# Reordering the even block's mixer: the recurrence's projections first, the attention beside the recurrence

## The chip, the cores and the metric

The kernel runs on one core of one Trainium2 chip, in one launch. The metric is the device time of a launch in microseconds (us), from the core's own clock. The profile is of one execution; its views give times from the start of that execution's span.

## The reference, cut to what matters

The program is a stack of blocks on 256 tokens of width 1024, in float32: a first block (attention beside a state-space mixer, then a feed-forward over 16384 experts), then two further layers. The change touches the mixer of the first of those two, the "even" one:

```python
def even_mixer(h, h_ctx, w_in, w_out, rpb, lb, hg_norm_w, with_ctx_out):
    na_q, na_k, na_v, hg_q, hg_ff, hg_fb, hg_i, hg_g = jnp.split(h @ w_in, EV_SPLITS, axis=-1)
    cna_q, cna_k, cna_v, chg_q, chg_ff, chg_fb, chg_i, chg_g = jnp.split(h_ctx @ w_in, EV_SPLITS, axis=-1)
    a_lat = neighbourhood_attention(nh(na_q), nh(na_k), nh(na_v), nh(cna_k), nh(cna_v), rpb)
    g_lat, g_ctx = hgrn2_mixer(hg_q, (hg_ff, hg_fb), hg_i, hg_g,
                               chg_q, (chg_ff, chg_fb), chg_i, chg_g, lb, hg_norm_w, with_ctx_out)
    y = jnp.concatenate([a_lat.reshape(b, s, NA_WIDTH), g_lat], axis=-1) @ w_out
```

So one wide projection (1024 to 4096 columns, in eight slices of 512) of the tokens `h` and of a 256-token context `h_ctx` feeds two branches that do not need each other: an attention of 8 heads of 64 (each query sees a window of the tokens plus all of the context), and a gated linear recurrence of 4 heads of 128, run once forward and once backward (d = 0 and 1). Both branches' outputs, side by side, go through the output projection.

## The kernel before, in words

**Projections.** Weights come from memory in units of 512 KB (128 rows x 1024 float32). Each unit is split into a high part (ScalarE, L217) and a low part (VectorE, every third one GpSimd, L222), and each product is three passes of matmuls, high by high, high by low and low by high (L227 to L229). `ev_in(c0, puts)` (L1409) does one 512-column slice that starts at column c0: two loads of two units each, and for each load and each source (`h`, or `hc` for the context) two groups of 24 matmuls of 256 columns; after each such pair of groups it yields. A slice wanted of both sources yields four times, a slice wanted of `h` alone twice. Group results leave PSUM (two buffers named mm) by the function `put`: a copy, a gate (`gate_T`: ScalarE tanh, VectorE L1402), or a silu (L1407).

The slices by their first column: 0 attention query (naq), 512 attention key (done ahead of the order that changes, with `first_T`), 1024 attention value, 1536 recurrence query (hq), 2048 and 2560 forget gates forward and backward, 3072 recurrence value (iv, civ), 3584 output gate (gN).

**Attention.** `nattn` (L1431) is a generator of 16 tiles, 8 heads by 2 halves of the tokens. A tile has scores (matmuls L1452, L1453), a bias added from PSUM to the tile s (L1455), a maximum (L1458), ScalarE's exponential (L1460), a reciprocal (L1461), four transposes (L1468), their copy to pT (L1470), the product with the values (L1474), and a scaling (L1475). Each head's bias is read by four DMAs of 64 KB on GpSimd's queue into braw, one buffer (L1441), and masked on GpSimd into bias, two buffers (L1443).

**Recurrence.** `prep` (L1533) makes, for each direction d and each pair of heads pc, the decays: logarithm, a scan along time (L1503), differences, exponentials and products (L1508 to L1518), and 8 transposes (L1529). `hgrn` (L1549) then works through 8 steps, head by head and in each head d = 0 and 1: `states` (matmuls L1557, L1570, L1573, VectorE L1559 and two scans L1577 of 512 columns) and, one step later, `outputs` of the step before (matmuls L1597 and 32 small ones L1602; after d = 1 also a normalisation: some 12 small VectorE operations from L351 on, and L1616). `by_chunk` (L1583) spreads a head's values on GpSimd (L1588) into two tiles that carry the attention's names s and pT, so they share the attention's two buffers each.

**Output projection.** `out_att(tt)` (L1673) starts the sum for half tt of the tokens from the residual (L1676) and adds the attention's four units `ua`; the recurrence's four units `ub` come last, with the next norm. Both halves' sums stay in PSUM (four buffers named acc, which the attention's scores and values and the recurrence's states use too). Units of the output weights are first multiplied by a gate row on GpSimd (L275).

**What sets the order.** Every engine has one queue and works it in order. The order written in the program gives priorities; a planner lays out each engine's queue from them with its own estimate of when operands and buffers are ready, so an instruction that is written later can stand ahead of one that would wait (the attention's first scores stand among the value projections that are written before them). SyncE's queue carries the weight loads, GpSimd's the bias loads.

The order written before: slices 0 and 1024 complete; then slices 2048, 3072, 2560, 1536 and 3584, sixteen yields, with one or two attention tiles after each of the first twelve, the decays after yields 4 to 6 and 12 to 15, and the first two recurrence steps after yields 14 and 15. At yield 11 the attention is finished, and its tiles naq and nak (and cnak, cnav) are reused for the transposed mixer outputs mixA and mixH. The other six recurrence steps follow with `out_att(0)` among them, then `out_att(1)` and the rest:

```python
    for i, _ in enumerate(units):
        for _ in range(2 if i % 3 == 2 else 1):
            next(na, None)
        if 4 <= i <= 6 or i >= 12:
            next(pr, None)
```

Of the kernel before, what the change touches and what calls it, by code (L numbers as in the profile page):

```python
# [8 lines left out]
F32 = mybir.dt.float32  # L9
F32R = mybir.dt.float32r  # L10
# [7 lines left out]
D = 1024  # L18
# [66 lines left out]
def program(tc, I, out, C, taps=None, upto=99):  # L85
# [1306 lines left out]
    def copy_T(dst, scale=1.0):  # L1392
        def put(ps, i):
            S.activation(dst[:, i], ps, AF.Copy, scale=scale)
        return put

    def gate_T(d, which):
        def put(ps, i):
            o = F[:, d, i // 2, which, i % 2]
            S.activation(o, ps, AF.Tanh, scale=0.5)  # L1400
            j = d * 4 + i
            V.tensor_scalar(o, o, lbc[:, 2, j:j + 1], lbc[:, 1, j:j + 1], op0=OP.mult, op1=OP.add)  # L1402
        return put
# [5 lines left out]
    def ev_in(c0, puts, natural=False):  # L1409

        for pc in range(2):
            un = load_up(Wev, c0 + pc * 256)
            for hsrc, put in puts:
                for u in range(2):
                    ps = ps_mm()
                    if natural:
                        up_N(un, u, hsrc, ps)
                        put(ps, u, slice(pc * 256, pc * 256 + 256))
                    else:
                        up_T(un, u, hsrc, ps)  # L1420
                        put(ps, pc * 2 + u)
                yield

    def copy_N(dst):
        return lambda ps, tt, cs: S.activation(dst[:, tt, cs], ps, AF.Copy)
# [123 lines left out]
    def hgrn(mixH):  # L1549
        def states(hd, d):  # L1550
            pc, hh = hd // 2, hd % 2
            kdl, kdc = KD[d, pc]
            kk, qe = F[:, d, pc, 0, hh], LF[d][:, pc, 1, hh]
            pa = ps_tr((128, 2, 128))
            for tt in range(2):
                ts = slice(tt * 128, tt * 128 + 128)
                P.matmul(pa[:, tt], kk[:, ts], qe[:, ts], start=True, stop=True)  # L1557
            at_ = atb[d][hd % 2]
            V.copy_predicated(at_, mdir[d].unsqueeze(1).to_broadcast([128, 2, 128]), pa)  # L1559

            st_ = []
            et = wrk.tile([128, 512], F32, name="et")
            S.activation(et.rearrange("p (v n) -> p v n", n=8), tots[d][pc][:, hh].unsqueeze(1).to_broadcast([128, 64, 8]),
                         AF.Exp)
            for vh in range(2):
                vs = slice(hd * 128 + vh * 64, hd * 128 + vh * 64 + 64)
                pm = ps_acc()
                pu = pm.rearrange("p (v n) -> p n v", n=8)
                for tt in range(2):
                    P.matmul(pu[:, 0], kdc[:, tt, hh], civ[:, tt, vs], start=tt == 0, stop=tt == 1)  # L1570
                for m, tt in enumerate((1, 0) if d else (0, 1)):
                    im = ivm[hd][tt][:, vh * 64:vh * 64 + 64]
                    P.matmul(pm.rearrange("p (v n) -> p v n", n=8)[:, :, 4 * m + 1:min(4 * m + 5, 8)], kdl[:, tt, hh],  # L1573
                             (im[:, :, 3:0:-1] if m else im[:, :, ::-1]) if d else (im[:, :, 0:3] if m else im),
                             start=True, stop=True)
                sv = wrk.tile([128, 512], F32, name="sv", bufs=3)
                V.tensor_tensor_scan(sv, et, pm, 0.0, op0=OP.mult, op1=OP.add)  # L1577
                st_.append(sv.rearrange("p (v n) -> p n v", n=8))
            return hd, d, at_, st_, qe

        oN, ivm, last_out = {}, {}, hg_out

        def by_chunk(hd):  # L1583

            ivm[hd] = []
            for tt, name in enumerate(("s", "pT")):
                t = wrk.tile([128, 512], F32, name=name).rearrange("p (v n) -> p v n", n=4)
                G.tensor_tensor(t, iv[:, tt, hd * 128:hd * 128 + 128].unsqueeze(2).to_broadcast([128, 128, 4]),  # L1588
                                rmask.unsqueeze(1).to_broadcast([128, 128, 4]), op=OP.mult)
                ivm[hd].append(t)  # L1590

        def outputs(hd, d, at_, st_, qe):
            if d == 0:
                oN[hd] = ps_mm((128, 2, 128))
            o = oN[hd]
            for tt in range(2):
                P.matmul(o[:, tt], at_[:, tt], iv[:, tt, hd * 128:hd * 128 + 128], start=d == 0 and tt == 0, stop=False,  # L1597
                         skip_group_check=True)
            for vh in range(2):
                for n in range(8):  # L1600
                    tt, i = n // 4, n % 4
                    last_out[0] = P.matmul(  # L1602
                             o[32 * i:32 * i + 32, tt, vh * 64:vh * 64 + 64], qe[:, n * 32:n * 32 + 32],
                             st_[vh][:, 7 - n if d else n], start=False, stop=d == 1 and vh == 1 and n == 7,
                             skip_group_check=True, tile_position=(0, 32 * i))
            if d == 0:
                return
            ss = wrk.tile([128, 2], F32, name="ss4")
            scr = wrk.tile([128, 512], BF, name="junk")
            for tt in range(2):  # L1610
                S.activation(scr[:, 0:128], o[:, tt], AF.Square, accum_out=ss[:, tt:tt + 1])
            rsqrt(ss, 1.0 / 128, 4 * EPS)
            cs = slice(hd * 128, hd * 128 + 128)
            ms = slice(512 + hd * 128, 640 + hd * 128)
            for tt in range(2):
                V.scalar_tensor_tensor(mixn[:, tt, ms], o[:, tt], ss[:, tt:tt + 1], gN[:, tt, cs], op0=OP.mult, op1=OP.mult)  # L1616

        last = None
        by_chunk(0)
        for hd in range(4):  # L1620
            if hd < 3:
                by_chunk(hd + 1)
            for d in range(2):
                if hd % 2 == 0:
                    queries(d, hd // 2)
                new = states(hd, d)
                if last:
                    outputs(*last)
                    if d == 0:
                        nat_T(lambda tt, c: mixn[:, tt, (4 + hd - 1) * 128:(4 + hd) * 128],  # L1630
                              [t[:, hd - 1:hd] for t in mixH], 1)
                last = new
                yield
        outputs(*last)
        yield True
        nat_T(lambda tt, c: mixn[:, tt, 896:1024], [t[:, 3:4] for t in mixH], 1)
# [1 line left out]
    first_T(1, hc, cnak)  # L1638
    first_T(0, h, nak)
    first_T(1, h, nak)  # L1640
    for g in (ev_in(0, [(h, copy_T(naq, 0.125))]),
              ev_in(1024, [(hc, copy_N(cnav)), (h, copy_N(nav))], True)):
        for _ in g:
            pass
    na, pr = nattn(), prep()
    units = itertools.chain(
        ev_in(2048, [(hc, gate_T(0, 1)), (h, gate_T(0, 0))]),
        ev_in(3072, [(hc, copy_N(civ)), (h, copy_N(iv))], True),
        ev_in(2560, [(hc, gate_T(1, 1)), (h, gate_T(1, 0))]),
        ev_in(1536, [(h, lambda ps, i: silu(hq[:, i], ps))]),  # L1650
        ev_in(3584, [(h, gate_N)], True))
    hg = mixA = None
    hg_out = [None]
    for i, _ in enumerate(units):
        for _ in range(2 if i % 3 == 2 else 1):
            next(na, None)
        if 4 <= i <= 6 or i >= 12:
            next(pr, None)
        if i == 11:
            for _ in na:  # L1660
                pass
            mixA = (mt([128, 4, T], "naq", F32R), mt([128, 4, T], "nak", F32R))
            mixH = (mt([128, 4, T], "cnak", F32R), mt([128, 4, T], "cnav", F32R))
            hg = hgrn(mixH)
        if i == 14:
            nat_T(lambda tt, c: mixn[:, tt, c * 128:(c + 1) * 128], mixA, 4)
        if i >= 14:
            next(hg)
    Weo = I["ev_w_out_2"][0]
    ua = load_dn(Weo, 0, grow, 4)  # L1670
    acc = [None, None]
# [7 lines left out]
            yield  # L1679

    o0 = out_att(0)
    for i, tail in enumerate(hg):
        if i < 6:
            next(o0, None)
        if i == 2:
            hh2, hl2 = mt([128, 2, D], "hh", F32R), mt([128, 2, D], "hl", F32R)
            ub = load_dn(Weo, 4, grow, 4, [(hh2[:, 0], hl2[:, 0]), (hh2[:, 1], hl2[:, 1])])
        if i == 6:
            for _ in o0:
                pass  # L1690
        if tail:
            with tc.issue_after(hg_out[0].ins):
                for _ in out_att(1):
                    pass
# [44 lines left out]
```

## Time and profile before

| what | value |
|---|---|
| median of 3 runs | 2160.7 us (2158.08 to 2161.99) |
| the profiled execution's own time | 2161.18 us |
| its span, first to last instruction | 2159.4 us |
| TensorE matmul busy | 2058.1 us (95%) |
| VectorE busy | 1607.4 us (74%) |
| ScalarE busy | 1030.4 us (48%) |
| GpSimd busy | 795.1 us (37%) |
| mean granted TensorE clock | 0.983 |

Reading: PE is TensorE's matmuls, PEld its weight loads, DVE VectorE, ACT ScalarE, POOL GpSimd, SP SyncE. L12 is line 12 of the kernel. Matmuls are pipelined, so the busy time of PE counts overlapping durations, and the distance from start to start says more about its pace. The mixer in question runs from about 1365 to 1645 us of the span.

### The profile page before, as it was taken

How to read it: one execution, taken by the hardware profiler on the slowest of the kernel's cores; microseconds unless marked ns; L12 is line 12 of the kernel's file. 1: busy time of each engine (PE TensorE's matmuls, PEld its weight loads, DVE VectorE, ACT ScalarE, POOL GpSimd, SP SyncE). 2: the span in 40 equal slices, each digit the busy share in tenths (PEclk: the TensorE clock that was granted, in tenths of full speed). 3: DMA queues.
4: the chain of work that ended last, by engine and by line, in shares of the span. 5: the costliest groups of instructions: out<-in, count | busy, mean ns of one | idle time of the engine just before them, and what ended most of it. 6: DMA issues, size and time to landing. Idle time of an engine off the chain costs nothing.

```text
span 2159.4 us, 37426 instructions
## 1 busy us (share of the span) xinstructions
PE 2058.1 (95%) x14726; PEld 1898.8 (88%) x14726; DVE 1607.4 (74%) x2576; ACT 1030.4 (48%) x1732; POOL 795.1 (37%) x392
## 2 busy tenths in 40 slices
PE   8999999999879999999999999999888999899999
PEld 7989999889879999997777777899876999798998
DVE  6677688779999346758997787536785877777877
ACT  5655565454434444444444555435524545445454
POOL 2221333113957876550000000323441556343554
PEclk9999999999989999999999999999999999899999
DMA  6544544456645766559998888746224655554552
GB/s 218 159 127 135 169 128 128 133 201 200 220 138 189 231 211 189 173 174 328 349 331 318 314 280 256 166 97 76 89 69 141 194 199 181 181 171 144 193 182 98
DMA packets 122035, 403.56 MB, mean 187 GB/s; under 512 B 14561, under 2 KB 23793, under 8 KB 121858
## 3 DMA queue, kind: packets, MB, share of 16 engines
q1 hardware_dynamic: 110688, 388.43, 54.4%
q0 software_dynamic: 1520, 3.75, 2.7%
q10 hardware_dynamic: 9650, 8.99, 1.2%
q8 instruction: 115, 1.88, 0.4%
q14 instruction: 62, 0.51, 0.1%
HBM read 390.56 MB, written 10.55 MB: 186 GB/s over the span
## 4 chain that ended last, share of the span: by engine, by line
PE 68%; DVE 17%; DMA 8%; issue 3%; ACT 3%; POOL 0%; SPq 0%; DVEq 0%; ACTq 0%; POOLq 0%
PE mm L227 15%; PE mm L228 14%; PE mm L229 14%; PE acc L309 4%; PE acc L312 4%; PE acc L308 4%; DMA xdt<-in_ada_w 3%; DMA wraw<-in_peer_v 3%; DVE A L180 3%; DVE wlo L1064 3%; PE tr L1019 1%; PE acc L1019 1%; DVE wlox L222 1%; DVE wlo L222 1%; ACT whi L1063 1%
## 5 line engine op out<-in xcount | busy, mean ns | idle before, releaser
L1043 POOL TENSOR_TENSOR wlo<-wraw,whi 128x1024 fp32r<-128x1024 f32 x126 | 321.3, 2555 | 182.6 <-ACT whi L1042 182.4
L227 PE MATMUL mm<-xdt,whi 128*128 128x256 f32 x1248 | 360.7, 290 | 7.1 <-ACT A L1055 5.7
L229 PE MATMUL mm<-xdt,wlo 128*128 128x256 f32 x1248 | 355.0, 285 | 0.6 <-POOL wlo L1043 0.6
L228 PE MATMUL mm<-xdt,whi 128*128 128x256 f32 x1152 | 327.9, 285 | 0.2 <-DVE xdt L418 0.2
L1042 ACT ACTIVATE whi<-wraw 128x1024 fp32r<-128x1024 f32 x128 | 135.7, 1060 | 236.0 <-PE mm L228 152.2
L227 PEld LDWEIGHTS mm<-xdt,whi 128*128 128x128 f32 x1248 | 240.5, 193 | 8.6 <-ACT A L1055 6.3
L229 PEld LDWEIGHTS mm<-xdt,wlo 128*128 128x128 f32 x1248 | 241.0, 193 | 1.4 <-POOL wlo L1043 1.2
L228 PEld LDWEIGHTS mm<-xdt,whi 128*128 128x128 f32 x1152 | 223.1, 194 | 0.4 <-DVE xdt L418 0.4
L222 POOL TENSOR_TENSOR wlo<-wraw,whi 128x1024 fp32r<-128x1024 f32 x37 | 93.8, 2538 | 308.4 <-ACT whi L217 271.6
L1063 ACT ACTIVATE whi<-wraw 128x1024 fp32r<-128x1024 f32 x128 | 134.6, 1057 | 106.8 <-DMA wraw<-in_peer_v 100.5
L1064 DVE TENSOR_TENSOR wlo<-wraw,whi 128x1024 fp32r<-128x1024 f32 x128 | 155.5, 1220 | 23.1 <-ACT whi L1063 22.9
L222 DVE TENSOR_TENSOR wlo<-wraw,whi 128x1024 fp32r<-128x1024 f32 x87 | 134.9, 1551 | 46.7 <-ACT whi L217 46.3
L227 PE MATMUL mm<-F,whix 128*128 128x256 f32 x560 | 158.6, 284 | 7.1 <-ACT whix L217 5.0
L217 ACT ACTIVATE whi<-wraw 128x1024 fp32r<-128x1024 f32 x124 | 130.7, 1055 | 71.9 <-PE mm L228 42.4
L228 PE MATMUL mm<-F,whix 128*128 128x256 f32 x560 | 158.5, 283 | 0.4 <-DVE F L418 0.4
L229 PE MATMUL mm<-F,wlox 128*128 128x256 f32 x560 | 158.2, 283 | 0.5 <-DVE wlox L222 0.5
L309 PE MATMUL acc<-wlo,wwh 128*128 128x512 f32 x512 | 149.9, 395 | 6.6 <-DVE wlo L1064 6.4
L312 PE MATMUL acc<-whi,wwl 128*128 128x512 f32 x512 | 147.2, 394 | 5.6 <-DVE wwl L222 5.4
L308 PE MATMUL acc<-whi,wwh 128*128 128x512 f32 x512 | 141.5, 393 | 5.5 <-ACT whi L1063 5.2
L275 POOL TENSOR_TENSOR wrawx<-wrawx,grow 128x1024 f32<-128x1024 f32 x38 | 107.0, 2828 | 90.5 <-DMA wrawx<-in_ffn_w_down 47.0
L1382 POOL MEMSET att<- 128x256 f32 x4 | 1.2, 312 | 358.2 <-DVE xdt L180 358.2
L309 PEld LDWEIGHTS acc<-wlo,wwh 128*128 128x128 f32 x512 | 95.5, 189 | 32.3 <-DVE wlo L1064 12.6
(619 smaller groups left out, 6321.6 us busy)
## 6 DMA issues: line engine op xcount, KB each, us to landing
wraw<-in_peer_u SPq DMA_DIRECT2D x128, 512.0 KB
wraw<-in_peer_v SPq DMA_DIRECT2D x128, 512.0 KB
xdt<-in_ada_w SPq DMA_DIRECT2D x72, 512.0 KB
wraw<-in_ffn_w_up SPq DMA_DIRECT2D x56, 512.0 KB
wraw<-in_w_in SPq DMA_DIRECT2D x42, 512.0 KB
wrawx<-in_ffn_w_up SPq DMA_DIRECT2D x32, 512.0 KB
wrawx<-in_ffn_w_down SPq DMA_DIRECT2D x31, 512.0 KB
wrawx<-in_w_in SPq DMA_DIRECT2D x30, 512.0 KB
```

The source lines that it names most:

```text
L217: S.activation(hi, raw, AF.Copy)
L222: eng.tensor_tensor(lo, raw, hi.bitcast(F32), op=OP.subtract)
L227: P.matmul(ps, ah, bh, start=start, stop=False)
L228: P.matmul(ps, ah, bl, start=False, stop=False)
L229: P.matmul(ps, al, bh, start=False, stop=stop)
L308: P.matmul(acc[tt][hf], ah, hi[:, fs], start=st_, stop=False, skip_group_check=free)
L309: P.matmul(acc[tt][hf], ah, lo[:, fs], start=False, stop=False, skip_group_check=free)
L312: P.matmul(acc[tt][hf], al, hi[:, fs], start=False, stop=sp_ and not free, skip_group_check=free)
L1042: S.activation(hi, raw, AF.Copy)
L1043: (G if b in POOL_U else V).tensor_tensor(lo, raw, hi.bitcast(F32), op=OP.subtract)
L1063: last_hi[0] = S.activation(hi, raw, AF.Copy)
L1064: V.tensor_tensor(lo, raw, hi.bitcast(F32), op=OP.subtract)
```

## The change

The slices are written in another order: 2048, 2560, 3072, 1024, 1536, 0, 3584, so that what the recurrence needs comes first, and the attention's query last but one. That is 22 yields (0 to 21). The decays stand after yields 4, 6, 8 and from 16 on; the first two recurrence steps stand after yields 19 and 21. The attention starts only behind the projections: four times one recurrence step and four attention tiles. Then the attention's output is transposed, and the last two recurrence steps run with `out_att(0)` between them; `ub` is loaded right behind `ua`.

Three things go with it. `by_chunk` gets tiles of its own (iv0, iv1), in place of the attention's s and pT. mixH lies in the tile of the context's low part (hcl), in place of cnak and cnav. And the room that is set aside for the descriptors of GpSimd's DMAs is set to 4096 bytes of each partition.

```diff
-            for tt, name in enumerate(("s", "pT")):
-                t = wrk.tile([128, 512], F32, name=name).rearrange("p (v n) -> p v n", n=4)
+            for tt in range(2):
+                t = wrk.tile([128, 512], F32, name=f"iv{tt}").rearrange("p (v n) -> p v n", n=4)
...
-    for g in (ev_in(0, [(h, copy_T(naq, 0.125))]),
-              ev_in(1024, [(hc, copy_N(cnav)), (h, copy_N(nav))], True)):
-        for _ in g:
-            pass
     na, pr = nattn(), prep()
-    units = itertools.chain(
...
+    for i, _ in enumerate(itertools.chain(
+            ev_in(2048, [(hc, gate_T(0, 1)), (h, gate_T(0, 0))]),
+            ev_in(2560, [(hc, gate_T(1, 1)), (h, gate_T(1, 0))]),
+            ev_in(3072, [(hc, copy_N(civ)), (h, copy_N(iv))], True),
+            ev_in(1024, [(hc, copy_N(cnav)), (h, copy_N(nav))], True),
+            ev_in(1536, [(h, lambda ps, i: silu(hq[:, i], ps))]),
+            ev_in(0, [(h, copy_T(naq, 0.125))]),
+            ev_in(3584, [(h, gate_N)], True))):
+        if 4 <= i < 10 and i % 2 == 0 or i >= 16:
+            next(pr, None)
+        if i == 18:
+            mixH = mt([128, 2, 4, T], "hcl", F32R)
+            mixH = (mixH[:, 0], mixH[:, 1])
+            hg_out = [None]
+            hg = hgrn(mixH)
+        if i >= 19 and i % 2:
+            next(hg)
+    for _ in pr:
+        pass
+    for i in range(4):
+        next(hg)
+        for _ in range(4):
             next(na, None)
...
+    for _ in na:
+        pass
+    mixA = (mt([128, 4, T], "naq", F32R), mt([128, 4, T], "nak", F32R))
+    nat_T(lambda tt, c: mixn[:, tt, c * 128:(c + 1) * 128], mixA, 4)
     Weo = I["ev_w_out_2"][0]
     ua = load_dn(Weo, 0, grow, 4)
...
     o0 = out_att(0)
-    for i, tail in enumerate(hg):
-        if i < 6:
-            next(o0, None)
-        if i == 2:
-            hh2, hl2 = mt([128, 2, D], "hh", F32R), mt([128, 2, D], "hl", F32R)
-            ub = load_dn(Weo, 4, grow, 4, [(hh2[:, 0], hl2[:, 0]), (hh2[:, 1], hl2[:, 1])])
-        if i == 6:
+    hh2, hl2 = mt([128, 2, D], "hh", F32R), mt([128, 2, D], "hl", F32R)
+    ub = load_dn(Weo, 4, grow, 4, [(hh2[:, 0], hl2[:, 0]), (hh2[:, 1], hl2[:, 1])])
+    for tail in hg:
+        next(o0, None)
+        next(o0, None)
+        if tail:
             for _ in o0:
                 pass
-        if tail:
             with tc.issue_after(hg_out[0].ins):
...
-    nc = bacc.Bacc("TRN2", target_bir_lowering=False, num_devices=1)
+    nc = bacc.Bacc("TRN2", target_bir_lowering=False, num_devices=1, dynamic_dma_scratch_size=4096)
```

## Rows read from the trace of the kernel before

**Rows 1.** Busy time by stretch: us; PE, PEld, DVE, ACT, POOL busy (count); granted clock, DMA share, GB/s

```profile
1420.00:1430.00 10.00, 10.00 (x86) 10.00 (x85) 0.52 (x1) 2.46 (x5) 2.14 (x1) 1.00 0.33 105
1450.00:1540.00 90.00, 89.72 (x692) 83.21 (x690) 55.80 (x91) 47.62 (x85) 23.74 (x25) 1.00 0.49 71
1540.00:1590.00 50.00, 37.47 (x250) 34.72 (x249) 47.95 (x46) 20.64 (x34) 38.78 (x20) 0.90 0.38 119
1590.00:1637.00 47.00, 45.50 (x465) 37.13 (x464) 31.54 (x83) 10.19 (x29) 3.49 (x3) 1.00 0.03 10
```

**Rows 2.** Who waited for whom, 1375 to 1650 us: total, times, longest

```profile
PE mm L227 <- DVE hq L1407: 3.6, 2, 3.3
PE tr L1529 <- DVE e L1515: 3.6, 1, 3.6
```

**Rows 3.** Line L227 alone, by stretch: PE and PEld busy (count)

```profile
1450.00:1540.00 90.00, 46.45 (x160) 30.18 (x160) 1.00 0.49 71
```

**Rows 4.** The chain that ended last, 1360 to 1680 us: start, us, what

```profile
1440.95 0.84 PE acc L1474 x8
...
1447.54 0.63 PE acc L1452 x2
1448.17 0.43 PE acc L1453 x2
...
1454.09 0.44 PE tr L1468 x4
...
1590.95 0.44 PE tr L1557 x4
...
1598.19 0.39 PE acc L1570 x4
1598.58 0.81 PE acc L1573 x4
...
1608.84 1.07 PE mm L1602 x32
...
1630.90 1.91 PE acc L1676 x4
...
1637.91 0.47 PE acc L312 x2
```

**Rows 5.** VectorE's groups by line, 1370 to 1660 us: busy, mean ns, idle before

```profile
L222 DVE TENSOR_TENSOR wlo<-wraw,whi 128x1024 fp32r<-128x1024 f32 x19 | 28.9, 1519 | 18.9 <-ACT whi L217 18.9
L1577 DVE TENSOR_TENSOR_SCAN sv<-et,acc 128x512 f32<-128x512 f32 x16 | 19.3, 1214 | 4.3 <-PE mm L1602 3.5 <-PE acc L1573 0.6
...
L1470 DVE COPY pT<-tr 128x512 f32<-128x512 f32 x16 | 10.9, 683 | 1.8 <-PE tr L1468 1.7
L1458 DVE TENSOR_REDUCE nm<-s 128x1 f32<-128x512 f32 x16 | 10.8, 678 | 1.5 <-ACT s L1456 1.4
L1455 DVE TENSOR_TENSOR s<-acc,bias 128x256 f32<-128x256 f32 x16 | 6.7, 419 | 3.3 <-PE acc L1453 3.3
L1475 DVE TENSOR_SCALAR n<-acc,sm 128x64 f32<-128x64 f32 x16 | 4.5, 279 | 11.3 <-PE acc L1474 11.3
L1461 DVE RECIPROCAL sm<-sm 128x1 f32<-128x1 f32 x16 | 2.6, 160 | 7.1 <-ACT s L1460 7.1
```

**Rows 6.** VectorE in order of time, 1597 to 1602 us: start, us, what

```profile
1597.57 0.14 DVE L351 TENSOR_SCALAR ss<-ss 128x2 f32<-128x2 f32 x1
...
1600.94 0.61 DVE L1616 SCALAR_TENSOR_TENSOR n<-mm,ss,gN 128x128 f32<-128x128 f32 x2
```

**Rows 7.** Line L1515 alone: duration ns min/median/max, first and last start

```profile
L1515 DVE TENSOR_TENSOR e<-e,F x4: 1225/2462/3357, 1470.1 to 1571.5; 128x1024 f32<-128x1024 f32 x4
```

**Rows 8.** The tile braw: duration ns min/median/max, first and last start; landing

```profile
L1441 POOL DMA_DIRECT2D braw<-in_na_rpb x32: 619/619/631, 1361.4 to 1501.3; - x32
L1443 POOL TENSOR_TENSOR bias<-braw,win x8: 1279/1282/1286, 1373.9 to 1511.1; 128x512 f32<-128x512 f32 x8
...
DMA to landing us min/median/max: 4.1/7.2/10.4
```

More of the change, by code (lines that the diff above doesn't have):

```diff
@@ L1640, in program @@
     first_T(1, h, nak)
-    for g in (ev_in(0, [(h, copy_T(naq, 0.125))]),
-              ev_in(1024, [(hc, copy_N(cnav)), (h, copy_N(nav))], True)):
-        for _ in g:
-            pass
     na, pr = nattn(), prep()
-    units = itertools.chain(
[L1647 to L1655, printed above, removed]
-            next(na, None)
[L1657 to L1668, printed above, removed]
+    for i, _ in enumerate(itertools.chain(
[20 more added lines that the diff above has]
+        for _ in range(4):
+            next(na, None)
+    for _ in na:
+        pass
+    mixA = (mt([128, 4, T], "naq", F32R), mt([128, 4, T], "nak", F32R))
+    nat_T(lambda tt, c: mixn[:, tt, c * 128:(c + 1) * 128], mixA, 4)
     Weo = I["ev_w_out_2"][0]
```

## The prediction

> **What bounds the kernel now.** I read the busy times by stretch first. From 1391 us (the end of the key projection, where the order begins to differ) to 1540 TensorE is full: 1420 to 1430 shows what full is, 86 starts of projection matmuls in 10 us, 0.116 us each, and 1450 to 1540 shows it with attention tiles and half the decays mixed in [rows 1]. Those 90 us hold 3 x 160 projection matmuls [rows 3], 55.8 us, and the other 212 instructions are 12 attention tiles and 16 transposes with four strays. At the prices of the chain [rows 4] a tile is 0.63 + 0.43 + 0.44 + 0.84 = 2.34 us, 28.1 us for 12, and the transposes 1.8 us: 85.7 of 90 us, so TensorE works at 95%. VectorE is busy for 62% there.
>
> Then it turns over. [...] The waits name it: TensorE waits 3.6 us for VectorE's silu of hq and 3.6 us for its product in the decays [rows 2]. [...] From 1590 to 1637 neither is full of work: the recurrence steps follow one another, VectorE at 67%, and TensorE's 45.5 busy us contain overlapping durations. Priced as below, its work there (8 sets each of L1557, L1597 and L1602, 10 pairs of L1570 and L1573, 51 matmuls like L312, 6 of L1676) is 42.5 us, 90%. The last matmul of `out_att(1)` ends at 1638.4 [rows 4]. So VectorE's work is badly spread: little before 1540, too much after.
>
> **The change part by part.** Nothing is removed or added in arithmetic; the sum is the length of the stretch from 1391 to 1638.4, now 247.4 us, in three parts.
>
> *Projections.* 22 yields of 48 matmuls at 0.116 us are 122.8 us. Beside them stand all 32 decay transposes (3.5 us at L1468's price), two `states` and one `outputs`. A `states` is 0.44 + 2 x (0.39 + 0.81) = 2.84 us of TensorE; an `outputs` is 0.44 (L1597, four of the form of L1557) + 1.07 = 1.51 [rows 4]. Together 133.5 us; at the 95% above 140.5, to 1531.5. VectorE's work for these (splits, gates, four decays) filled 62% or less of the like stretch; the backward decays need the last context product, at yield 14, and have eight yields of 5.6 us to run in before the end. What covers them is that room; if they came late, the stalls of [rows 2] would return, 7 us. Weight loads: the last six yields take 6 MB in 34 us, of which the four raw buffers can hold 2 MB beforehand; the other 4 MB are 119 GB/s, what 1540 to 1590 moved at 0.38 of the DMAs' time [rows 1]. I take no stall.
>
> *Attention beside four recurrence steps.* TensorE: 16 x 2.34 + 4 x 4.35 = 54.8 us, 57.7 at 95%. VectorE [rows 5]: a tile is 0.42 + 0.68 + 0.16 + 0.68 + 0.28 = 2.22 us, 35.5 for 16; four `states` at 2 x 1.21 + 0.42 (L1559, taken at L1455's price: as many columns from PSUM) are 11.4; two normalisations from 1597.57 to 1601.55 with a scan of 1.2 between, 2.8 each [rows 6], 5.6; two query products at 0.68 (512 columns, as L1458), up to 2.5 each beside GpSimd; four splits of `ua` at 1.52, 6.1. That is 60 us bare. The attention's and the scans' operations, which read PSUM or one SBUF operand, are not slowed by GpSimd in the trace; for the others I add 3.6 us: 63.6, and at the 96% busy that VectorE reached from 1540 to 1590, 66 us. Ends: 57.7 (TensorE alone at 95%) and 73 (TensorE at its 75% of 1540 to 1590). I take 66, because VectorE's sum is the larger. To 1597.5. A tile that slips in among the last projections costs there what it saves here, and is not counted.
>
> *The tail.* Two `states` and three `outputs`, 10.2 us; 16 transposes for mixA and mixH, 1.8; both `out_att`: 48 matmuls at 0.235 and eight of the residual, 3.8 [rows 4], 15.1. Sum 27.1; at the 90% of 1590 to 1637, 30 us. To 1627.6. The ends are 27 and 36 (TensorE at 75%).
>
> The sum is 236.6 against 247.4: 10.8 us less. What comes behind (the recurrence's output units, the norm) only moves along.
>
> *Small parts.* The tiles of `by_chunk` are what lets steps and attention overlap; their GpSimd work is the same. mixH in the context's tile waits for yield 14's products, which are long done. The smaller room for descriptors could at worst make each of GpSimd's loads wait for the one before, 4 x 7.2 us a head in place of 4 x 0.62 [rows 8]; four loads are outstanding at most, as before, and no row shows an issue that waited, so I take 0 and leave a chance for it. At the start, GpSimd's bias loads before the first split may be gone or not: 0 to 1.5 us of gain, taken as 0.
>
> A sentence on the clock: the stretch from 1590 to 1637, all small matmuls and transposes, was granted 1.00 [rows 1]. [...]
>
> **The rivals.**
> *A, no change.* The two branches are chained through the same four acc buffers, freed by VectorE in queue order; TensorE then gets no more than its 75% in the last two parts: 73 + 36 = 109 in place of 96, the end at 1640, 2163 us. For it: TensorE and VectorE are both near full. Against: at 95% with attention among projections they shared those buffers too.
>
> *B, slower: the bias loads become the bound.* braw is one buffer, so a head's bias takes four issues, the landing and the mask: 2.5 + 7.2 + 1.3 = 11.0 us at the median, 7.9 to 14.2 by the landing's ends [rows 8]. Now the eight masks are spread over 1373.9 to 1511.1, some 20 us apart; behind the change eight heads get 66 us, 8.2 each. Two masked heads and one raw lie ready; the mask of head 2 comes when head 0 is done, 8.2 us in, and head 7's is then 8.2 + 5p, wanted at 57.7 us. At p = 11.0 it is 5.5 us late, at 14.2 it is 21.5 late: 2172 us. It decides from p = 12.1, where it eats the 10.8 us. `ua`'s gate products in GpSimd's queue add to p. Against it: the DMAs have little else to do, so landings should lie at the short end.
>
> *C, better: everything overlaps.* 97% on TensorE in the first part, 58 us in the second, 28 in the tail: 2139 us. For it: VectorE has room during the last projections.
>
> [...]
>
> That the change doesn't reorder what it says isn't likely: every engine works its queue in order, though the planner, not the written order, has the last word on how far the attention moves.
>
> **How the numbers follow.** Forecast 0.51, A 0.16, B 0.19, C 0.12, D 0.02. The profiled execution took 2161.18 us, span 2159.4 and 1.8 around it, 0.5 above the median of 2160.7. Less 10.8 it is 2150.4; I give 2151. Range: the forecast's own ends run from 2142 (the second part at its lower end) to 2156; A reaches 2163, and the milder half of B, up to a period of 12.8, adds 14.5 to the forecast, 2165; C is mostly below. 2140 to 2166 leaves out D, half of B and most of C. What a measurement can tell here is about 0.2%, 4.3 us: faster below 2156.4, slower above 2165. Faster: forecast and C, 0.63; same: A, 0.16; slower: B and D, 0.21.
>
> **What would show it.** Right: projections back to back from 1391 to about 1531, with all four L1503 scans inside; no stretch of 50 us with VectorE at 96% while TensorE is below 80%; L1515 nearer 1.2 us; attention scores L1452 among recurrence L1573 up to some 1597; the last `out_att` at about 1628. Wrong by A: TensorE idle behind pT, sv or s in the middle part. Wrong by B: GpSimd's L1443 waiting for braw instead of for L1455, and L1455 waiting for bias. A stall for hq or the splits before 1531 would say that the cover of the decays failed.

## The result, and the profile after

The changed kernel took 2187.7 us (median of 4, 2180.47 to 2194.48) against 2159.39 us (median of 4): a ratio of 1.0132 with a 95% interval of 1.0089 to 1.0176. It is slower by 1.3%, where 2151 us was forecast. The profiled execution took 2194.48 us, span 2192.7, granted clock 0.971; it is the longest of the four, which took 2180.47, 2182.71, 2192.69 and 2194.48 us at mean clocks of 0.980, 0.978, 0.973 and 0.971.

The first part ended when forecast. TensorE in order of time, in the kernel after: the last matmul of a projection stands at 1532.3 us, where 1531.5 was forecast.

```profile
1532.32 0.28 PE L229 MATMUL mm<-whi,hl 128*128 128x256 f32 x1
1532.44 0.61 PE L1597 MATMUL mm<-iv,att 128*128 128x128 f32 x4
```

Busy time by stretch, in the columns of [rows 1]:

```profile
1450.00:1532.00 82.00, 81.32 (x659) 79.24 (x658) 45.84 (x46) 39.50 (x61) 33.80 (x16) 1.00 0.37 117
1540.00:1590.00 50.00, 33.61 (x167) 26.49 (x168) 30.59 (x62) 9.28 (x25) 20.61 (x21) 0.58 0.47 47
1590.00:1637.00 47.00, 43.87 (x243) 35.34 (x242) 24.17 (x60) 11.73 (x31) 8.69 (x11) 0.68 0.28 12
1540.00:1650.00 110.00, 89.33 (x454) 71.88 (x455) 59.81 (x133) 22.98 (x61) 29.30 (x32) 0.61 0.35 31
```

TensorE is full to 1532, with VectorE at 56%. Then two things are to be seen. From 1540 to 1590 VectorE is busy for 30.59 of 50 us, not the 47.95 of [rows 1], so the heap of VectorE's work is gone, as meant; but TensorE issued 167 instructions in place of 250. And the granted clock is 0.58 and 0.68. Read in stretches of 2 us from 1540 to 1650, it is 1.00 or 0.50, and between them (0.70 to 0.94) only where it goes from one to the other. With these as the upper and the lower level, a mean of 0.61 over 110 us is, as an estimate, 2 x 0.39 x 110 = 86 us at the lower one; the kernel before, at 0.95 over the same stretch, had 11.

TensorE's waits from 1375 to 1680 us (total, times, longest), the counterpart of [rows 2], show one that is new:

```profile
PE tr L450 <- DVE n L1616: 13.3, 1, 13.3
PE acc L1474 <- DVE pT L1470: 7.3, 10, 0.8
PE mm L1602 <- DVE sv L1577: 2.7, 3, 1.8
...
PE tr L1529 <- DVE e L1515: 1.1, 2, 0.8
```

The waits for hq and e have shrunk to 0.4 and 1.1 us. The new one is a stop of 13.3 us behind the first normalisation. VectorE in order of time there (start, us), beside [rows 6], where L351 took 0.14 us:

```profile
1541.09 2.31 DVE L351 TENSOR_SCALAR ss<-ss 128x2 f32<-128x2 f32 x1
1543.43 0.65 DVE L354 TENSOR_SCALAR rq<-ss 128x2 int32<-128x2 int32 x1
...
1544.32 0.16 DVE L357 SCALAR_TENSOR_TENSOR rq<-ry 128x2 f32<-128x2 f32 x1
1544.51 6.63 DVE L358 TENSOR_TENSOR rq<-rq,ss 128x2 f32<-128x2 f32 x1
1551.06 1.21 DVE L222 TENSOR_TENSOR hl<-wraw,hh 128x1024 fp32r<-128x1024 f32 x1
...
1552.58 0.16 DVE L358 TENSOR_TENSOR rq<-rq,ss 128x2 f32<-128x2 f32 x1
```

and GpSimd in the same microseconds, without a gap:

```profile
1540.01 3.36 POOL L275 TENSOR_TENSOR wraw<-wraw,grow 128x1024 f32<-128x1024 f32 x1
1543.33 0.72 POOL L1429 TENSOR_TENSOR gN<-gN,nw 128x256 f32<-128x256 f32 x1
1544.00 2.46 POOL L1441 DMA_DIRECT2D braw<-in_na_rpb  x4
1546.47 2.35 POOL L275 TENSOR_TENSOR wrawx<-wrawx,grow 128x1024 f32<-128x1024 f32 x1
1548.77 2.35 POOL L275 TENSOR_TENSOR wraw<-wraw,grow 128x1024 f32<-128x1024 f32 x1
```

L358 multiplies two elements a partition. It ends at 1551.14, within 0.02 us of the end of GpSimd's last gate product, and 6.63 us is 41 times what it takes at 1552.58. The transposes L450 and L1468, on TensorE's queue behind it, waited, to 1554.04 and 1554.31.

Last, the clock. Six stretches between 1555 and 1650 us, in the same columns:

```profile
1555.00:1574.00 19.00, 17.55 (x62) 14.29 (x61) 7.22 (x15) 2.78 (x7) 3.73 (x5) 0.50 0.27 13
...
1583.00:1598.00 15.00, 14.22 (x51) 11.50 (x50) 6.57 (x24) 2.71 (x8) 5.33 (x8) 0.50 0.64 27
1600.00:1609.00 9.00, 8.22 (x76) 6.29 (x74) 5.54 (x13) 3.22 (x8) 3.10 (x5) 1.00 0.20 13
1610.00:1622.00 12.00, 12.00 (x43) 10.46 (x44) 4.57 (x10) 2.01 (x5) 1.27 (x1) 0.50 0.36 14
1623.50:1629.00 5.50, 5.03 (x57) 3.82 (x56) 4.04 (x15) 2.72 (x9) 0.00 (x0) 1.00 0.01 3
1630.00:1649.50 19.50, 17.58 (x66) 14.28 (x66) 7.64 (x22) 3.94 (x10) 0.00 (x0) 0.50 0.08 27
```

The chain that ended last, from 1605 to 1631:

```profile
1605.06 0.60 PE tr L1468 x4
...
1605.69 0.70 DVE pT L1470
...
1606.44 1.10 PE acc L1474 x8
...
1608.60 0.60 PE tr L1468 x4
...
1609.23 0.70 DVE pT L1470
...
1609.97 1.97 PE acc L1474 x8
...
1618.60 1.60 PE acc L1573 x4
...
1624.35 0.44 PE tr L1468 x4
...
1628.57 0.70 DVE pT L1470
...
1629.32 1.78 PE acc L1474 x8
```

Two attention tiles in a row sent their transposes and then waited 0.70 us for the copy to pT; L1474 behind the second is at the lower level, 1.97 us for the 1.10 of 3.5 us before. From there to 1622.5 the chain stays on TensorE without a wait, with a recurrence step in it at double price (L1573 1.60 against 0.81 of [rows 4]), and L1468 at 1624.35 is at the upper level again. At 1628.6 a wait for pT stands in the chain once more, and from 1630 the clock is at 0.50. So in this trace the clock falls among attention tiles and comes back with each recurrence step, at about 1575, 1599, 1623 and 1650. Of the 86 us at the lower level some 34 run from the stop at 1541 to the end of the next recurrence step, at 1574.6; the other 50, in three stretches that begin at 1582, 1610 and 1629.5, follow on waits for pT of 0.8 us at most, with no stop before them.

### The profile page after: what moved, and what is told of

It reads as the page before. It is cut to its first block, busy times and chain, and to the rows that moved or that the text cites. A ratio compares the mean times of both kernels' runs of the same rounds, so it can differ in the third digit from the quotient of the medians.

```text
span 2192.7 us, 37443 instructions
## 1 busy us (share of the span) xinstructions
PE 2081.4 (95%) x14726; PEld 1914.7 (87%) x14726; DVE 1600.8 (73%) x2576; ACT 1030.1 (47%) x1732; POOL 793.6 (36%) x392
## 4 chain that ended last, share of the span: by engine, by line
PE 72%; DVE 16%; DMA 5%; issue 3%; ACT 3%; POOL 0%; SPq 0%; DVEq 0%; ACTq 0%; POOLq 0%
PE mm L227 14%; PE mm L228 14%; PE mm L229 14%; PE acc L309 5%; PE acc L312 5%; PE acc L308 5%; DVE A L180 3%; DMA xdt<-in_ada_w 3%; DVE wlo L1064 2%; DMA wraw<-in_peer_v 1%; PE acc L1019 1%; PE tr L1019 1%; PE acc L1474 1%; DVE wlox L222 1%; PE acc L1573 1%
## 5 line engine op out<-in xcount | busy, mean ns | idle before, releaser
L227 PE MATMUL mm<-xdt,whi 128*128 128x256 f32 x1248 | 359.8, 290 | 7.2 <-ACT A L1055 5.8
L227 PEld LDWEIGHTS mm<-xdt,whi 128*128 128x128 f32 x1248 | 239.5, 192 | 8.7 <-ACT A L1055 6.4
L227 PE MATMUL mm<-F,whix 128*128 128x256 f32 x560 | 158.0, 283 | 5.7 <-ACT whix L217 4.2
L312 PE MATMUL acc<-whi,wwl 128*128 128x512 f32 x512 | 147.1, 393 | 4.1 <-DVE wwl L222 4.1
L275 POOL TENSOR_TENSOR wrawx<-wrawx,grow 128x1024 f32<-128x1024 f32 x38 | 104.9, 2775 | 90.6 <-DMA wrawx<-in_ffn_w_down 65.8
```

The lines of the kernel that those rows point to most:

```text
L227: P.matmul(ps, ah, bh, start=start, stop=False)
L312: P.matmul(acc[tt][hf], al, hi[:, fs], start=False, stop=sp_ and not free, skip_group_check=free)
```

## The experiments

Two theories. **The stop**: GpSimd's gate products block the normalisation, TensorE stands for 13 us, and the clock falls from there. **The thin part**: without projections among them the attention tiles leave TensorE a wait each, and the clock falls with or without a stop. The expectations call the first theory 1 and the second rival 2. The table has all kernels; the clock is that of 1540 to 1650, the microseconds at the lower level, 0.50, are estimated as 2 x (1 - clock) x 110, and L415 opens what follows the mixer. That column also holds when an execution reached the mixer (1376 us before, 1372 after, 1370.5 to 1380 in the experiments), and in the faster kernels the stretch to 1650 reaches past the mixer.

| kernel | median, us | ratio to before, 95% | clock | us at 0.50 | L415 starts |
|---|---|---|---|---|---|
| before | 2159.1 to 2160.6 | 1 | 0.95 | 11 | 1647.1 |
| after | 2187.7 | 1.0132 [1.0089, 1.0176] | 0.61 | 86 | 1684.5 |
| e1 before, small descriptor room | 2160.51 | 1.0 [0.9985, 1.0015] | 0.92 | 18 | 1647.6 |
| e2 after, gate products late | 2184.16 | 1.0123 [1.0082, 1.0163] | 0.71 | 64 | 1673.3 |
| e3 after, filler | 2166.7 | 1.0028 [1.0016, 1.004] | 0.92 | 18 | 1656.9 |
| e4 after, both | 2164.56 | 1.0022 [1.0006, 1.0037] | 0.92 | 18 | 1650.1 |
| e5 after, gate products on VectorE | 2181.81 | 1.0108 [1.0084, 1.0132] | 0.77 | 51 | 1670.4 |
| e6 e5 with the filler | 2160.97 | 1.0011 [0.9998, 1.0024] | 0.94 | 13 | 1650.5 |
| e7 before, own iv tiles | 2156.67 | 0.9985 [0.997, 1.0] | 0.95 | 11 | 1639.2 |
| e8 before, decays early | 2146.07 | 0.9932 [0.9909, 0.9956] | 0.97 | 7 | 1634.1 |
| e9 before, filler | 2161.68 | 1.0008 [0.999, 1.0026] | 0.95 | 11 | 1653.8 |
| e10 after, half the tiles beside projections | 2161.82 | 1.0007 [0.999, 1.0023] | 0.86 | 31 | 1648.8 |
| e11 e8, one step earlier | 2153.19 | 0.9954 [0.9936, 0.9971] | 0.95 | 11 | 1642.4 |

### e1: the descriptor room alone

```diff
-    nc = bacc.Bacc("TRN2", target_bir_lowering=False, num_devices=1)
+    nc = bacc.Bacc("TRN2", target_bir_lowering=False, num_devices=1, dynamic_dma_scratch_size=4096)
```

> The kernel before with the smaller room for DMA descriptors alone. Theory 1 (the loss is a stop of TensorE at 1540 us, made by GpSimd's gate products, and the low clock after it): no change, 2159 us within 4. Rival 3 (the smaller room slows GpSimd's loads): braw issues longer than 631 ns and the kernel slower.

2160.51 us, ratio 1.0. The room is not a cause.

### e2: the gate products behind the last bias mask

```diff
-            G.tensor_tensor(bias.rearrange("p t (r c) -> p (t r) c", r=4),
+            masks[:] = [G.tensor_tensor(bias.rearrange("p t (r c) -> p (t r) c", r=4),
...
-    ua = load_dn(Weo, 0, grow, 4)
+    with tc.issue_after(masks[0].ins):
+        ua = load_dn(Weo, 0, grow, 4)
```

and the same for `ub`.

> The changed kernel with GpSimd's eight gate products of the output weights queued behind the last bias mask, so that none of them stands beside the first normalisation at 1541 us. Theory 1 (the stop takes the clock down): the stop of 13 us shrinks to 2 or 3, the granted clock stays at 1.00 through the attention, and the time is 2150 to 2156 us. Rival 2 (the attention without projections beside it is too thin for the clock by itself): the stop goes, 2194 less some 11 us, but the clock still reads 0.50 from some 1555 us on: 2172 to 2183 us.

The stop at 1541 falls to 3.5 us, but the time only from 2187.7 to 2184.2, with overlapping intervals. TensorE's waits on pT have grown to 16.3 us, the longest 7.0: the products have met the next normalisation instead. VectorE of e2, in order of time (the long instructions):

```profile
1608.99 2.30 DVE L351 TENSOR_SCALAR ss<-ss 128x2 f32<-128x2 f32 x1
...
1611.47 2.12 DVE L354 TENSOR_SCALAR rq<-ss 128x2 int32<-128x2 int32 x1
...
1613.84 2.05 DVE L355 TENSOR_SCALAR ry<-rq 128x2 int32<-128x2 int32 x1
1615.81 0.68 DVE L1472 COPY pT<-tr 128x512 f32<-128x512 f32 x1
```

and GpSimd of e2 beside them:

```profile
1604.65 3.34 POOL L275 TENSOR_TENSOR wrawx<-wrawx,grow 128x1024 f32<-128x1024 f32 x1
1607.95 7.92 POOL L275 TENSOR_TENSOR wraw<-wraw,grow 128x1024 f32<-128x1024 f32 x3
```

What the stop showed is seen a second time in another place, operations of the normalisation at 2.05 to 2.30 us beside gate products: moved, the products still cost. The time is just above the range of the thin part, 2172 to 2183, and 28 us above the other's. The clock was at the lower level for 64 us although the first stop was short: 20 us follow on that stop and some 31 on the second, but two stretches of 6 to 7 us, from 1574 and from 1595, follow on waits of 1.3 us at most. Those two speak for the thin part.

### e3: filler for TensorE

Five bf16 matmuls of 256 columns of zeros in each attention tile, ahead of the product that waits for pT; nothing uses their result.

```diff
-            o = ps_acc((128, 64))
+            o = ps_acc()
+            for _ in range(5):
+                P.matmul(o[:, 256:512], zeros[:, 0:128], zeros, start=True, stop=True)
+            o = o[:, 0:64]
```

> The changed kernel with five more matmuls of zeros (256 columns, bf16) in each of the 16 attention tiles, ahead of the products that wait for pT; their results are not used. The gate products stay where they are. Theory 1 and rival 2 both expect the 13 us stop to remain; with the fill the clock comes back to 1.00 within some 10 us after it, and 40 to 70 us of work at half clock shrinks: 2155 to 2170 us. If the waits for pT are the bound and not the clock, the time stays at 2180 to 2195 us.

2166.7 us: 21 us of the loss are back from work that computes nothing. The stop is still there, 12.2 us, and the clock falls at it; from 1563 on it stays up. Busy time by stretch of e3:

```profile
1540.00:1590.00 50.00, 36.43 (x286) 29.20 (x286) 39.47 (x73) 13.73 (x35) 27.82 (x27) 0.83 0.57 59
1590.00:1637.00 47.00, 47.00 (x349) 38.24 (x348) 26.81 (x69) 12.20 (x34) 5.00 (x6) 1.00 0.23 21
```

With such a stop and without the filler, in the changed kernel, the clock from 1590 to 1637 is 0.68; here it is 1.00, and the waits for pT have fallen from 7.3 to 0.6 us. So the falls that no stop precedes are the thin part's. Whether the filler holds the clock by filling the waits or by being more matmuls is not separated.

### e4: filler and late gate products

Both edits, e2's and e3's.

> Both: the gate products behind the last bias mask, and the five matmuls of zeros in each tile. Theory 1: as e2, the fill adds nothing or costs up to 9 us (80 matmuls of 0.11 us): 2150 to 2162 us. Rival 2: clearly faster than e2 by the clock, 2150 to 2160 us against 2172 to 2183.

2164.56 us, not told from e3 (the intervals overlap). It is above both expected ranges. The clock is 1.00 from 1540 to 1590 and falls to 0.82 in 1590 to 1637, behind a wait of 3.3 us, while the late gate products run. Late or early, a wait of TensorE stands beside them, and behind this one the clock fell although the filler was in.

### e5: gate products on VectorE

```diff
-                    G.tensor_tensor(raw, raw, gate, op=OP.mult)
+                    (eng or G).tensor_tensor(raw, raw, gate, op=OP.mult)
...
-    ua = load_dn(Weo, 0, grow, 4)
+    ua = load_dn(Weo, 0, grow, 4, eng=V)
```

and the same for `ub`.

> The changed kernel with the eight gate products of the output weights on VectorE in place of GpSimd, so that GpSimd has nothing long to do beside the normalisations. Theory 1 (a stop takes the clock down): no wait of TensorE over 5 us, the clock at 1.00, 2150 to 2160 us. Rival 2 (the attention without projections beside it is too thin for the clock): no long wait either, yet the clock at 0.5 to 0.75 from some 1550 us on, 2172 to 2185 us.

L358 alone in e5 (duration in ns: min, median, max):

```profile
L358 DVE TENSOR_TENSOR rq<-rq,ss x12: 151/161/163, 1550.3 to 1654.7; 128x2 f32<-128x2 f32 x12
```

Without the products on GpSimd no L358 is long any more, so they were what held it. A wait of 7.7 us remains, where 5 at most was expected: VectorE now has the products in its own queue, and the first L351 starts at 1546.8 in place of 1541.1. The time is 2181.8, in the range of the thin part; the 6 us to the changed kernel are not clear of the noise, as the intervals overlap. The clock goes up and down, 51 us of 110 at the lower level. Some 31 of them run from this wait to 1572; the other 19 follow on waits of 0.8 us at most, which is the thin part. But such waits do not always take the clock down. From 1597 to 1629 six tiles waited 0.34 to 0.79 us for pT, and busy time by stretch of e5 has the upper level there:

```profile
1600.00:1610.00 10.00, 8.09 (x49) 6.13 (x49) 6.28 (x16) 2.78 (x7) 3.71 (x5) 1.00 0.59 21
1610.00:1620.00 10.00, 9.22 (x84) 7.43 (x84) 7.46 (x21) 3.54 (x11) 1.27 (x1) 1.00 0.10 7
1620.00:1630.00 10.00, 7.53 (x48) 5.77 (x47) 7.11 (x21) 3.59 (x9) 0.00 (x0) 0.99 0.00 0
```

What decides it is not shown.

### e6: e5 with the filler

> The same with five matmuls of zeros in each attention tile. Both theories: clock 1.00 throughout and no long stop; what is left is VectorE's and TensorE's own work, 2148 to 2158 us (4 to 10 us under the filled kernel with the stop, 2166.7). If it stays at 2162 to 2168, the stop was not worth its 13 us, and the attention's own chain is what bounds the part.

2160.97 us, above the 2148 to 2158 expected: level with before, not faster. Busy time of e6 from 1540 to 1590, and from 1590 to 1637:

```profile
1540.00:1590.00 50.00, 43.18 (x332) 34.41 (x332) 35.01 (x86) 12.60 (x34) 15.29 (x20) 0.86 0.54 60
1590.00:1637.00 47.00, 47.00 (x368) 38.33 (x367) 26.30 (x70) 10.83 (x32) 3.66 (x5) 1.00 0.18 18
```

TensorE is full, the filler included, and 5.6 us of stop and 13 us of low clock are left at the beginning.

### e9: the filler in the kernel before

> The kernel before with the same filler as in e3 (five matmuls of 256 columns of zeros per attention tile, whose results nothing uses). It prices the filler where the clock is at its upper level anyway. If the filler simply costs TensorE its own length, 16 x 5 x 0.11 us = 9 us are added (2168 to 2170, ratio 1.004) and e6's level time of 2161 hides a gain of the order itself. If the filler only fills time that TensorE would have waited, the time is 2159 to 2163 (ratio 0.999 to 1.002), and e6 is the whole worth of the new order at full clock. The 10 us at a lower clock between 1540 and 1590 could go in either case, for 3 us at most.

1.0008, which by the expectation makes e6 the new order's whole worth. The trace doesn't allow that reading alone: in e9 the stalls for hq and e of [rows 2], 7.2 us together, have shrunk to 2.8 for e and none over 1.1 for hq, and so the filler may be paid out of them. Its price in e6 lies between 0 and its own length, an estimated 9 us (80 matmuls at the 0.116 us of a projection's, which have as many columns). Whether the new order at full clock would be level or 9 us better stays open.

### e10: half of the attention beside projections

```diff
+            ev_in(0, [(h, copy_T(naq, 0.125))]),
             ev_in(1536, [(h, lambda ps, i: silu(hq[:, i], ps))]),
-            ev_in(0, [(h, copy_T(naq, 0.125))]),
...
+        if i >= 18:
+            for _ in range(2):
+                next(na, None)
...
-        for _ in range(4):
+        for _ in range(2):
             next(na, None)
```

> The changed kernel with eight of the sixteen attention tiles moved back beside the last four yields of projections (the attention's query slice one place earlier, two tiles behind each of the yields 18 to 21, then two tiles behind each of the four recurrence steps). Theory 'the part without projections is too thin for the clock': the part becomes half as long with as many recurrence steps in it, so the microseconds at the lower level between 1500 and 1650 fall from 85 to below 55 and the time to 2160 to 2172. Theory 'the stop of 13 us starts the fall' alone: the gate products of the output weights still meet the normalisations, the stop remains, the clock falls as before, and the time stays at 2180 to 2190.

2161.82 us, in the range that the thin part gave and 18 us below the other's. Busy time by stretch of e10:

```profile
1540.00:1650.00 110.00, 99.42 (x692) 80.15 (x691) 71.48 (x154) 32.44 (x80) 25.89 (x25) 0.86 0.29 42
```

From after to e10, 55 us of lower clock are gone, and 26 us of time. The edit also parted the normalisation from the gate products (no L358 above 0.162 us; the longest wait is 3.6 us, for a scan), so it does not price the two apart. But here real work does what the filler did.

### e7, e8 and e11: the same aim in the order before

If VectorE's heap behind the projections was the fault, the decays can go earlier without moving the attention. e7 takes only the tiles iv0 and iv1 over (with the smaller room, to make space):

> The kernel before with one part of the change: tiles of their own for the spread values (and the smaller room for descriptors that makes place for them). If the sharing with the attention held the recurrence back, 2 to 6 us less, 2154 to 2158 us; if VectorE was the bound from 1540 to 1590, no change, 2157 to 2163 us.

0.9985, an interval that reaches 1.0: a gain of 0 to 6.5 us. e8 leaves the iv tiles out, keeps the smaller room, gives the backward decays a tile of their own in place of hch, exchanges two slices and makes the decays at once:

```diff
-        LF[d] = mem.tile([128, 2, 2, 2, T], F32, name=("lf", "hch")[d])
+        LF[d] = mem.tile([128, 2, 2, 2, T], F32, name=("lf", "lfb")[d])
...
+        ev_in(2560, [(hc, gate_T(1, 1)), (h, gate_T(1, 0))]),
         ev_in(3072, [(hc, copy_N(civ)), (h, copy_N(iv))], True),
-        ev_in(2560, [(hc, gate_T(1, 1)), (h, gate_T(1, 0))]),
...
-        if 4 <= i <= 6 or i >= 12:
+        if 4 <= i <= 6 or 8 <= i <= 10:
             next(pr, None)
```

> The kernel before with its attention left among the projections, and only the backward gates' slice one place earlier, the backward decays in a tile of their own, and their work right behind (yields 8 to 10 in place of 12 to 15). If the spread of VectorE's work is worth what the prediction gave it, the stretch from 1540 to 1590 loses the decays' 15 to 20 us of VectorE and the time falls by 5 to 12 us, to 2148 to 2156 us, with the clock at 1.00. If VectorE's late work was not the bound, no change, 2157 to 2163 us.

2146.07 us, 0.9932: **faster than both kernels**, by 13 us than before. Busy time by stretch of e8:

```profile
1540.00:1590.00 50.00, 45.09 (x393) 40.43 (x393) 41.39 (x56) 17.86 (x32) 42.52 (x22) 0.97 0.38 127
1590.00:1637.00 47.00, 46.12 (x377) 36.97 (x375) 28.95 (x71) 14.99 (x36) 1.60 (x1) 1.00 0.08 24
```

and its L1515 alone, beside [rows 7]:

```profile
L1515 DVE TENSOR_TENSOR e<-e,F x4: 1216/1221/1227, 1470.0 to 1525.2; 128x1024 f32<-128x1024 f32 x4
```

The last decay product is at 1525 in place of 1571.5 and at its best price. From 1540 to 1590 VectorE has 6.6 us less to do, where 15 to 20 less were expected, and TensorE issues 393 instructions in place of 250, at a clock of 0.97. The gain is 1 us above the expected 5 to 12; the three parts of the edit were not run singly. e11 takes the first recurrence step forward as well (`i >= 13` for `i >= 14`):

> As e8 (the order before, with the decays early), and the first recurrence step behind yield 13 in place of 14, which the early decays allow. If what is left of VectorE's load behind the projections sets the end, one step of some 6 us of VectorE's work moves forward and the time falls to 2141 to 2145 (ratio 0.991 to 0.993 against before). If TensorE is the bound again, as 1450 to 1540 was, it stays at 2145 to 2148.

2153.19 us, above both expected ranges: no further gain, and the interval just overlaps e8's. Its trace has a wait of 4.1 us behind a normalisation and a clock of 0.93 from 1590 to 1637, where e8 has neither; that this is the 7 us between the two is not shown.

## Why the prediction was wrong

**Projections: right in the main, and partly by luck.** 1531.5 forecast, 1532.3 measured. But the profiled execution began the new order at 1386.8, 4 us before the 1391 that the forecast starts from, so the part took 145.5 us and not 140.5. TensorE's waits there come to 4.2 us, and the scores of two attention tiles stand in it. The backward decays fitted in: the waits for hq and e came to 1.5 us, and L1515 ran at 1.20 to 2.30.

**The middle part: wrong, and it decides.** 66 us were forecast, to 1597.5, as VectorE's sum at 96%; L1474 ended at 1646, 114 us. VectorE was busy for 59.81 of the 110 us from 1540, so it was not the engine that led. The step that failed is the sentence on the clock, that the stretch from 1590 to 1637 "was granted 1.00"; a lower clock in the last two parts, **rival D**, got 0.02. That stretch shows only that recurrence steps with output products between them kept the clock there. It has no attention tile in it. Nor is it "all small matmuls and transposes": by the prediction's own count 57 of its matmuls, like L312 and L1676, have 512 columns and take 15 of its 42.5 us. In the kernel before every tile had projections beside it, and [rows 1] had no stretch of attention and recurrence alone. The one near it, 1540 to 1590, stood at 0.90 and was not used: it was the part in which TensorE waited.

The failed sentence is also one of the sum: the ends of the middle part were 57.7 and 73 us, all at prices of [rows 4] taken at 1.00. In the low stretches L1468 cost 1.06 in place of 0.44, L1474 1.97 in place of 0.84, L1573 1.60 in place of 0.81. From 1532.4 to 1646.3 us TensorE worked for 90.6 us and waited for 23.3: 13.3 in the stop, 7.3 for pT and 2.7 for the scans. Of the 90.6, some 63 lie in stretches at the lower level. At half the pace, as an estimate by L1573's 1.60 for 0.81, 31 of them are lost, and 59 are left, near the 57.7 that the sum had for TensorE alone. So the work was priced rightly for 1.00, and what the sum left out are the clock, some 31 us, the stop, 13, and the waits for pT and the scans, 10. `out_att(1)` ended at 1673.5, 46 us behind the 1627.6 forecast.

No run shows D in full, the 82 us of TensorE's work in the last two parts (54.8 and 27.1) all at a lower clock: in the kernel after the clock came back to 1.00 with every recurrence step and was 1.00 from 1651 to 1674.

No run varies the transposes alone. In the chain they are 1.20 us of the 7.1 before the clock fell at 1610 and 1.90 of the 12.6 before it came back at 1622.5, 17 and 15%, so their share does not separate the stretches; in this trace the waits for pT do, though e5 has such waits at 1.00 as well.

**The stop: left out.** The sum took "two normalisations, 2.8 each"; the first took from 1541.09 to 1554.0, 12.9 us. Its 3.6 us for operations slowed by GpSimd left out those with one SBUF operand; L351, which has one, took 2.31 us in place of 0.14. [rows 7] had L1515, with two large SBUF operands, at 1.23 to 3.36 us, the longer ones where GpSimd was busy for 38.78 of 50 us [rows 1], and the text saw that `ua`'s gate products lengthen GpSimd's queue, but it looked for the damage in bias loads, not in VectorE's small operations. In the kernel before the normalisations stood where GpSimd did 3.49 us of work in 47.

**The tail: right.** 30 us forecast, 27.5 measured (1646 to 1673.5), at the lower level to 1650 and at 1.00 from there.

**The rivals.** A did not occur as put: the acc buffers were not what TensorE waited for. Its sign did occur, TensorE idle behind pT and sv, for 10 us. B did not occur: L1443 waited 36.9 us for VectorE to use a bias and 14.7 for braw, 8.3 of these ahead of the new order, and L1455 waited for TensorE alone; issues stayed at 617 to 640 ns, against 619 to 631 before. The descriptor room, taken at 0, measured 0. C's 2139 should be 2137 to 2138 by its own terms; nothing rests on it.

**What stays open.** At full clock and without the stop the order might yet be worth what was forecast, or nothing (e6, e9). The stop and the thin part were not priced apart to the microsecond: moving the gate products, which left other waits of 7.0 and 7.7 us, gave 3.5 to 6 us, not clear of the noise (e2, e5); filling alone gave 21 (e3), both 23 to 27 (e4, e6). In e6, at the upper level, L1443 waited 23.5 us for braw, so the bias loads of B come nearer there. The tile of mixH and the earlier load of `ub` were not run by themselves.

## What to carry to other kernels

When work is moved out from beside a dense stream, ask what the thinner stretch will be granted as a clock, and price it at both levels seen here, 1.00 and 0.50 (L1573: 0.81 and 1.60 us); a stretch of the profile vouches only for its own mix of work. Spread the overloaded engine's work into the dense part (e8, 13 us gained) before moving the dense part away (28 us lost). Before elementwise products go to GpSimd, look for chains of small VectorE operations that will run beside them (L358: 6.63 us in place of 0.16).

## What the runs showed of the hardware

L358, a VectorE operation on two elements a partition, took 6.63 us in place of 0.16 and ended with the second of two gate products on GpSimd, which make up 4.65 of these. The first 2 us lie beside the bias loads' issues; L357 took 0.16 us beside them, so what held L358 there is not shown. In e3, with the products still on GpSimd, the longest L358 took 6.63 us again; in e5, with the products off GpSimd, none took over 0.163. Operations with one SBUF operand were long as well: L351, L354 and L355 took 2.05 to 2.30 us in e2, beside three gate products that took 7.92 us together, 2.64 each. So the 6.63 us span two gate products, and the others are no longer than one.

Matmuls of zeros that nothing reads made the whole kernel 21 us faster (2187.7 to 2166.7), with the waits for pT down from 7.3 to 0.6 us and the time at the lower clock level from 86 to 18.
